# Two-layer HGRN2 and attention trunk in fp32r: the LayerNorms done by rows ahead of their transposes

## The chip, the cores and the metric

One core of one Trainium2 chip. The metric is the device time of one execution in microseconds (us). The kernel before takes 2177.33 us, the median of three runs (2177.27 to 2179.59).

## What is computed

The input x is one sequence of 1024 rows with 1024 channels in fp32. There are two layers. Each first mixes the rows (an HGRN2 recurrence in layer 0, sliding-window attention in layer 1), then applies a gated feed-forward network with 2816 hidden channels, and after both comes a residual with a LayerNorm:

```python
for layer in range(2):
    mix = hgrn2_mixer(h, ...) if layer == 0 else swa_sink_mixer(h, k_shared, v_shared, ...)
    h = layer_norm(ALPHA * h + mix, ln_mix_g[layer], ln_mix_b[layer])
    h = layer_norm(ALPHA * h + conv_ffn(h, ...), ln_ffn_g[layer], ln_ffn_b[layer])
    if layer == 0:
        k_shared, v_shared = split(h @ shared_w_kv)

def layer_norm(x, g, b):
    mu, var = x.mean(-1), square(x - mu).mean(-1)
    return (x - mu) * rsqrt(var + 1e-5) * g + b
```

So there are four LayerNorms: the mix norm and the end norm of either layer. g and b have one value for each channel.

## The kernel before, in words

Rows lie on partitions in eight blocks `tb` of 128 rows. The tile `Y` holds them as eight columns of 1024 channels. For a product the rows have to be turned: TensorE transposes each 128x128 piece into PSUM (L182), and the turned block is written to SBUF, with channels on partitions. Every fp32 product is done as three fp32r matmuls (L172 high x high, L173 with a low part of one operand, L174 with that of the other). `split` (L198) makes the two parts: a cast on ACT (L199) gives the high part and a subtraction on DVE (L147) the low part. A piece of weights costs the same two instructions.

The order of time is: the HGRN2 mixer; `out_proj` of layer 0 with the mix norm; `Up` (the first feed-forward product, 2 x 11 column pairs `fc`); `Down` (the second); keys and values; attention; then `out_proj`, `Up` and `Down` of layer 1. `Up` and `Down` use a Strassen-Winograd form with seven block products each, so DVE also forms sums of blocks of weights and of turned rows. TensorE runs in an order written out in the program; a list `od` of small tasks interleaves transposes with matmuls, each task due at a given matmul time. Inside keys, values and attention DVE, ACT and POOL are in written order too; elsewhere a scheduler orders them. SP issues nearly all transfers, in order.

**The mix norm, `out_proj` (L317) and `Up.ln` (L370).** `out_proj` makes the second 512 columns of the blocks in the order tb = 4, 5, 6, 7, 0, 1, 2, 3. For each block DVE adds the residual (L340), takes statistics (L213) and spawns `Up.ln`: L219 and L220 finish them, and POOL raises the variance to the power -1/2 (L221). Then the rows are normalised in place, without g and b: for tb 4 to 7 POOL forms -mu/sigma (L229, L230) and ACT applies it (L231), and for tb 0 to 3 DVE does it in two pieces (L235). SP stores the block to DRAM as `ynd` (L373). Eight matmul times later TensorE turns the block into two PSUM banks (L182), and ACT writes the turned block with eight activations of 128x128 (L247) that apply g and b, which are now one scalar per partition (`par`). The splits and Winograd sums of turned blocks follow. The weights of `fc` = 0 and 1 are split beforehand (`weight_load`, `weight_sums`); two of their pieces lie in the tile `HT`.

**The residual of the second norm.** `ynd` has no g and b, so `Down.run` (L638) loads g and b as rows broadcast over partitions (two transfers of 512 KB), reloads each `ynd` block and applies the rows on DVE with two instructions of 128x1024 per block (L645), sixteen in a layer, between Down's first products. Down's evacuations (L597, L601) add the products to it.

**The end norms.** In layer 0 `ln_mid` (L252) normalises a block with L235, turns it in two halves, and writes each half with two activations on ACT (L247) and two `tensor_scalar` on DVE (L249), which apply g and b; then it splits it into `T` for keys and values. The residual gets its g and b in the attention part by `ln_rows` (L263): 32 instructions of 128x512 on DVE (L268). In layer 1 `ln_last` (L273) writes the output with two `scalar_tensor_tensor` of 128x1024 for each block (L279: subtract mu, multiply by the row g; L282: multiply by 1/sigma, add the row b).

Of the kernel before, what the change touches and what calls it, by code (L numbers as in the profile page):

```python
# [85 lines left out]
def trunk(ctx: ExitStack, tc: tile.TileContext, a: dict, out: bass.AP):  # L86
# [25 lines left out]
    rbd = drp.tile([16, 2 * P], F32, name="rbd")  # L112
    bsd = [drp.tile([P, FF // 256, 2, D], F32, name=f"bsd{l}") for l in range(2)]
# [13 lines left out]
    tail, place = {}, {}  # L127
# [96 lines left out]
    def ln_normal(tb, on_scalar=False):  # L224
        y = Y[:, tb, :]
        mv, rs = ln_stats(tb)
        if on_scalar:
            ms = sm.tile([P, 1], F32, name="ms")
            nc.gpsimd.tensor_scalar(ms, mv[:, 0:1], -1.0, None, op0=ALU.mult)  # L229
            nc.gpsimd.tensor_tensor(ms, ms, rs, op=ALU.mult)  # L230
            nc.scalar.activation(y, y, AF.Identity, bias=ms, scale=rs)  # L231
            return
        for q in range(2):
            yq = y[:, q * 512:(q + 1) * 512]
            nc.vector.tensor_scalar(yq, yq, mv[:, 0:1], rs, op0=ALU.subtract, op1=ALU.mult)  # L235

    def ln_turn(tb, hf, gcol, bcol, banks, on_vector=0, halves=range(2)):

        for q in halves:
            ps = banks(q)  # L240
            for k in range(4):
                tr(ps[:, k * P:(k + 1) * P], Y[:, tb, (4 * q + k) * P:(4 * q + k + 1) * P])
            for k in range(4):
                kc = 4 * q + k
                shift, scale = par[:, bcol + kc:bcol + kc + 1], par[:, gcol + kc:gcol + kc + 1]
                if k < 4 - on_vector:
                    nc.scalar.activation(hf[:, kc, :], ps[:, k * P:(k + 1) * P], AF.Identity, bias=shift, scale=scale)  # L247
                else:
                    nc.vector.tensor_scalar(hf[:, kc, :], ps[:, k * P:(k + 1) * P], scale, shift,  # L249
                                            op0=ALU.mult, op1=ALU.add)  # L250

    def ln_mid(tb, gcol, bcol):  # L252
        ln_normal(tb)
        yield 11.0 if tb < 4 else 18.0
        hf = place["hf"](tb)
        for q in range(2):
            ln_turn(tb, hf, gcol, bcol, lambda _: psax()[:, :512], 2, (q,))
            if q == 0:
                yield 1.2
        ts = slice(tb * P, (tb + 1) * P)  # L260
        split(T[:, 0, :, ts], T[:, 1, :, ts], hf)

    def ln_rows(tbs, rows, wait, spill):  # L263
        for tb in tbs:
            for h in range(2):
                y = Y[:, tb, h * 512:(h + 1) * 512]
                for r, op in zip(rows, (ALU.mult, ALU.add)):
                    nc.vector.tensor_tensor(y, y, r[h], op=op)  # L268
                if h:
                    nc.sync.dma_start(spill[:, tb, :], Y[:, tb, :])  # L270
                yield wait

    def ln_last(tb, rows):  # L273
        y = Y[:, tb, :]
        mv, rs = ln_stats(tb)
        n = 1 if tb < NB - 1 else 2
# [4 lines left out]
        for hs in parts:  # L281
            nc.vector.scalar_tensor_tensor(y[:, hs], y[:, hs], rs, rows[1][:, hs], op0=ALU.mult, op1=ALU.add)  # L282
            nc.sync.dma_start(out[0, tb * P:(tb + 1) * P, hs], y[:, hs])
# [79 lines left out]
    class Up:  # L363
        def __init__(self, l, pool, rx):
            self.l, self.rx = l, rx
            self.wv = a["ffn_w_in"][l].rearrange("(kc p) c -> p kc c", p=P)
            self.TX = pool.tile([P, 3, 2, 4, 512], F32R, name="TX")
            self.W, self.raw, self.pieces = {}, {}, 0

        def ln(self, tb, gcol, bcol):  # L370
            with urgent():
                ln_normal(tb, tb > 3)
                nc.sync.dma_start(ynd[:, tb, :], Y[:, tb, :])  # L373
# [4 lines left out]
            with urgent():  # L378
                for q in range(2):
                    ln_turn(tb, hf, gcol, bcol, lambda _: psmm(), halves=(q,))  # L380
                    if tb < 4:
                        ks = slice(4 * q, 4 * q + 4)
# [21 lines left out]
        def weight_load(self, fc):  # L404
# [7 lines left out]
            for r in (r1, r2):  # L412
                j = self.pieces % (4 if fc > 1 else 3)
# [10 lines left out]
        def weight_sums(self, fc):  # L424
# [9 lines left out]
            split(blocks(2, 0), blocks(2, 1), r2)  # L434
# [50 lines left out]
        def run(self, ready, down):  # L485
# [7 lines left out]
            od.finish(ready[4:])  # L493
            mm = [psmm() for _ in range(4)]
# [25 lines left out]
    class Down:  # L520
# [117 lines left out]
        def run(self, mid_rows, end_rows, ln):  # L638
            self.later = []
            rows = row_tiles([self.free_rows(3 + j) for j in range(2)], *mid_rows)  # L640

            def shift(tb, r, op):
                if r is rows[0]:
                    nc.sync.dma_start(Y[:, tb, :], ynd[:, tb, :])
                tt(Y[:, tb, :], Y[:, tb, :], r, op=op)  # L645

            for tb in (0, 4, 1, 5, 2, 6, 3, 7):
                for r, op in zip(rows, (ALU.mult, add)):
                    self.later.append(lambda tb=tb, r=r, op=op: shift(tb, r, op))
            for i in range(7):  # L650
                for n, _ in enumerate(self.product(i, ln)):
                    if n % 4 == 3 and 44 * i + n > 8 and self.later:
                        self.later.pop(0)()
                    if i == 5 and n == 20 and end_rows is not None:
# [11 lines left out]
    with tc.tile_pool(name="t", bufs=1, reuse_waits="tile") as raws, hgrn_pool as hp:  # L666
# [48 lines left out]
        with tc.tile_pool(name="ep", bufs=1, reuse_waits="tile") as ep:  # L715
# [20 lines left out]
            with tc.manual_schedule(engines={EN.PE, EN.SP, EN.Activation, EN.DVE}):  # L736
                for i, n in enumerate(("hgrn_lb_logits", "ln_mix_g", "ln_mix_b", "ln_ffn_g", "ln_ffn_b")):
                    nc.scalar.dma_start(pr[16 * i:16 * (i + 1), :], a[n].rearrange("r (k p) -> (r k) p", p=P))
                nc.scalar.dma_start(pr[80:81, :], a["hgrn_gnorm_w"])
                nc.scalar.copy(warm, nhalf)  # L740
# [678 lines left out]
```

## Time and profile before

| | |
|---|---|
| median of three runs | 2177.33 us |
| the profiled execution's own time | 2176.27 us |
| its span in the trace | 2174.5 us |
| busy: PE / DVE / ACT / POOL | 2142.3 / 1735.6 / 917.1 / 186.2 us |
| granted TensorE clock | 0.999 |
| stages, roughly | layer 0 mixer to 470; out_proj and mix norm to 600; Up to 1000; Down to 1200; keys, values, attention to 1455; out_proj and mix norm to 1560; Up to 1950; Down to 2174.5 |

The engines are PE (TensorE matmul), DVE (VectorE), ACT (ScalarE), POOL (GpSimd) and SP (which issues transfers). A row of the groups gives a line of the program, its engine and operation, what is written from what, its shape and count, and behind the bar its busy time, the mean of one in ns, and the idle time before it with what ended it. A row of the waits reads: who waited <- for what: us in total, times, longest us. A row of the windows gives, for a stretch A:B, its length and then the busy time of PE, PEld, DVE, ACT and POOL, the granted clock, and the share and rate of the DMA.

### The profile page before, as it was taken

To read this page: it belongs to the slowest core of one execution; us is meant where nothing else is said; L and a number is where in the kernel's file an instruction comes from. 1 tells how busy PE (TensorE), PEld (TensorE's weight loads), DVE (VectorE), ACT (ScalarE), POOL (GpSimd) and SP (SyncE) were. 2 spreads that over 40 slices of the span, in tenths; PEclk is the share of its full clock that TensorE was granted. 3 is DMA by queue.
4 is the path that set the end of the run, shared out by engine and by line. 5 is a ranking of instruction groups with operands and counts; after the bars stand their busy time and mean duration, and the time that the engine had idled before them with its cause. 6 is when DMAs were issued, how large, how long until landed. Compare 5 with 4: busy or idle time off the path is not lost.

```text
span 2174.5 us, 32559 instructions
## 1 busy us (share of the span) xinstructions
PE 2142.3 (99%) x12879; PEld 1779.7 (82%) x12879; DVE 1735.6 (80%) x2281; ACT 917.1 (42%) x1535; POOL 186.2 (9%) x207
## 2 busy tenths in 40 slices
PE   8999999999999999999999999999999999999998
PEld 8788888878788888888888887778888888888887
DVE  3777666466789888889998766758899988889987
ACT  3333333243744443344443346755644444443431
POOL 0222121211100000000000022311000000000002
PEclk9999999999999999999999999999999999999999
DMA  5555443222222222228854331123133222249563
GB/s 198 194 195 180 151 175 121 69 88 93 90 80 91 84 78 87 87 97 270 291 170 136 106 100 35 35 97 117 59 109 96 87 79 76 79 163 327 198 216 128
DMA packets 225556, 278.97 MB, mean 128 GB/s; under 512 B 29721, under 2 KB 154362, under 8 KB 222586
## 3 DMA queue, kind: packets, MB, share of 16 engines
q1 hardware_dynamic: 224952, 276.76, 38.1%
q8 instruction: 101, 1.65, 0.3%
q14 instruction: 53, 0.43, 0.1%
q10 hardware_dynamic: 450, 0.12, 0.0%
HBM read 213.90 MB, written 62.93 MB: 127 GB/s over the span
## 4 chain that ended last, share of the span: by engine, by line
PE 77%; DVE 13%; DMA 3%; ACT 3%; issue 2%; POOL 1%; SPq 0%; ACTq 0%; DVEq 0%; POOLq 0%
PE psmm L172 16%; PE psmm L174 16%; PE psmm L173 16%; PE psax L172 7%; PE psax L174 7%; PE psax L173 7%; PE psax L178 3%; DVE T L147 2%; DVE HL L147 2%; PE psmm L178 2%; PE psax L1216 1%; PE psax L182 1%; DVE Y L477 1%; ACT T L199 1%; ACT Y L247 1%
## 5 line engine op out<-in xcount | busy, mean ns | idle before, releaser
L172 PE MATMUL psmm<-T,HL 128*128 128x512 f32 x896 | 358.2, 400 | 0.0
L173 PE MATMUL psmm<-T,HL 128*128 128x512 f32 x896 | 349.2, 390 | 2.8 <-DVE T L147 2.8
L174 PE MATMUL psmm<-T,HL 128*128 128x512 f32 x896 | 349.5, 390 | 0.0
L477 DVE SCALAR_TENSOR_TENSOR Y<-Y,cwt 128x1023 f32<-128x1023 f32 (+1 forms) x176 | 225.0, 1278 | 39.6 <-ACT Y L475 39.4
L475 ACT ACTIVATE Y<-Y,cwt 128x1024 f32<-128x1024 f32 x88 | 108.9, 1238 | 257.5 <-DVE Y L464 254.4
L173 PEld LDWEIGHTS psmm<-T,HL 128*128 128x128 f32 x896 | 168.6, 188 | 35.8 <-DVE T L147 3.5
L172 PEld LDWEIGHTS psmm<-T,HL 128*128 128x128 f32 x896 | 168.2, 188 | 36.1 <-issue 2.1
L174 PEld LDWEIGHTS psmm<-T,HL 128*128 128x128 f32 x896 | 168.1, 188 | 36.2
L199 ACT CAST HL<-rx 128x1024 fp32r<-128x1024 f32 (+1 forms) x137 | 140.4, 1046 | 113.1 <-DMA rx<-in_ffn_w_in_dram 31.4
L147 DVE TENSOR_TENSOR HL<-rx,HL 128x1024 fp32r<-128x1024 f32 (+1 forms) x137 | 165.4, 1210 | 12.9 <-ACT HL L199 12.3
L221 POOL TENSOR_TENSOR rs<-rs,nhalf 128x1 f32<-128x1 f32 x32 | 27.3, 854 | 1305.0 <-DVE rs L220 1304.7
L172 PE MATMUL psax<-T,HL 128*128 128x512 f32 x352 | 137.3, 390 | 0.0
L174 PE MATMUL psax<-T,HL 128*128 128x512 f32 x352 | 137.0, 389 | 0.0
L173 PE MATMUL psax<-T,HL 128*128 128x512 f32 x352 | 136.9, 389 | 0.0
L172 PE MATMUL psmm<-HL,T 128*128 128x256 f32 (+1 forms) x400 | 126.0, 315 | 0.0
L173 PE MATMUL psmm<-HL,T 128*128 128x256 f32 (+1 forms) x400 | 122.4, 306 | 1.0 <-DVE HL L147 0.9
L174 PE MATMUL psmm<-HL,T 128*128 128x256 f32 (+1 forms) x400 | 122.2, 306 | 0.1
L865 POOL TENSOR_TENSOR kp<-kp,tot 128x512 f32<-128x512 f32 x48 | 74.3, 1549 | 277.0 <-PE psax L178 139.9
L199 ACT CAST HT<-rx 128x1024 fp32r<-128x1024 f32 (+1 forms) x51 | 44.0, 862 | 88.5 <-PE psmm L173 29.9
L147 DVE TENSOR_TENSOR HL<-raw,HL 128x1024 fp32r<-128x1024 f32 x51 | 63.5, 1246 | 22.0 <-ACT HL L154 22.0
L172 PEld LDWEIGHTS psmm<-HL,T 128*128 128x128 f32 x400 | 76.9, 192 | 4.7 <-issue 1.2
L173 PEld LDWEIGHTS psmm<-HL,T 128*128 128x128 f32 x400 | 76.7, 192 | 4.8 <-DVE HL L147 1.7
(295 smaller groups left out, 5207.5 us busy)
## 6 DMA issues: line engine op xcount, KB each, us to landing
rx<-in_ffn_w_in_dram SPq DMA_DIRECT2D x136, 256.0 KB
rx<-gd SPq DMA_DIRECT2D x118, 256.0 KB
Y<-in_ffn_w_out_dram SPq DMA_DIRECT2D x44, 512.0 KB
bsd<-Y SPq DMA_DIRECT2D x22, 1024.0 KB
gd<-Y SPq DMA_DIRECT2D x44, 512.0 KB
raw<-in_hgrn_w_in_dram SPq DMA_DIRECT2D x32, 512.0 KB
rx<-in_ffn_w_out_dram SPq DMA_DIRECT2D x54, 256.0 KB
R<-bsd SPq DMA_DIRECT2D x44, 256.0 KB
```

Of the source, the lines that this page charges most:

```text
L147: make = lambda e: e.tensor_tensor(lo, src, hi.bitcast(F32), op=ALU.subtract)
L172: nc.tensor.matmul(ps, st(0), mv(0), start=start, stop=False)
L173: nc.tensor.matmul(ps, st(0), mv(1), start=False, stop=False)
L174: nc.tensor.matmul(ps, st(1), mv(0), start=False, stop=stop)
L178: nc.tensor.matmul(ps, lhsT, rhs, start=start, stop=stop, **kw)
L182: nc.tensor.transpose(ps, src, ident)
L199: nc.scalar.copy(hi, src)
L221: nc.gpsimd.tensor_tensor(rs, rs, nhalf, op=ALU.pow)
L247: nc.scalar.activation(hf[:, kc, :], ps[:, k * P:(k + 1) * P], AF.Identity, bias=shift, scale=scale)
L475: nc.scalar.activation(c, u, AF.Identity, bias=cwt[:, l, 3, ci:ci + 1], scale=cwt[:, l, 2, ci:ci + 1])
L477: nc.vector.scalar_tensor_tensor(c[:, sh:], u[:, :S - sh], cwt[:, l, 2 - sh, ci:ci + 1], c[:, sh:], op0=ALU.mult, op1=ALU.add)
L865: (nc.gpsimd if i else nc.vector).tensor_tensor(kv[:, :, 0, :], kv[:, :, 0, :], tv[:, :, 1:2].to_broadcast([P, nb, m]), op=ALU.mult)
```

## The change

All four norms go through one function, `ln_by_rows`: statistics as before, and then, while the block still has rows on partitions, two `scalar_tensor_tensor` of 128x1024 on DVE with g and b as broadcast rows (L238 and L241), and the store of the finished block: to `ynd`, to `h2d` or to the output. What is turned afterwards is finished, so ACT only copies it.

- At the start POOL issues two DRAM-to-DRAM transfers that copy ln_mix_g and ln_mix_b to `lmd`. `Up` loads its two rows from there into `HT` when it is made (two transfers of 512 KB on SP; in layer 1 they stand among the loads of the residual, ahead of those of the weights of `out_proj`).
- In `Up.ln` the instructions L229, L230, L231 and L235 go, and eight activations L247 give place to two copies of 128x512 (L345).
- `HT` holds the rows until the last block is normalised, so the last split of the weights of `fc` = 0 is put off (`self.last`) until after Up's products 4 and 5; the pieces of the raw weights are used in another order.
- In `Down.run` the row loads and L645 go; the eight reloads stay. The end norm's rows are loaded in product 5 in both layers.
- `ln_mid` turns a block in one piece of 128x1024 and splits it straight from PSUM; L247, L249, `ln_rows` with L268 and its row loads go.

TensorE's products are the same. The core of the diff:

```diff
-    def ln_normal(tb, on_scalar=False):
-        ...
-    def ln_turn(tb, hf, gcol, bcol, banks, on_vector=0, halves=range(2)):
-        ...
-    def ln_rows(tbs, rows, wait, spill):
-        ...
+    def ln_mid(tb):
+        yield 11.0 if tb < 4 else 18.0
+        ps = psax()
+        for kc in range(KC):
+            tr(ps[:, kc * P:(kc + 1) * P], Y[:, tb, kc * P:(kc + 1) * P])
+        ts = slice(tb * P, (tb + 1) * P)
+        split(T[:, 0, :, ts], T[:, 1, :, ts], ps.rearrange("p (k t) -> p k t", k=KC))
+
+    def ln_by_rows(tb, rows, dst, n=1):
         y = Y[:, tb, :]
         mv, rs = ln_stats(tb)
         parts = [slice(h * D // n, (h + 1) * D // n) for h in range(n)]
         for hs in parts:
             nc.vector.scalar_tensor_tensor(y[:, hs], y[:, hs], mv[:, 0:1], rows[0][:, hs],
                                            op0=ALU.subtract, op1=ALU.mult)
         for hs in parts:
             nc.vector.scalar_tensor_tensor(y[:, hs], y[:, hs], rs, rows[1][:, hs], op0=ALU.mult, op1=ALU.add)
-            nc.sync.dma_start(out[0, tb * P:(tb + 1) * P, hs], y[:, hs])
+            nc.sync.dma_start(dst[:, hs], y[:, hs])
...
             self.W, self.raw, self.pieces = {}, {}, 0
+            self.rows = [tail["R"][:, j, :].bitcast(F32) for j in range(2)]
+            for j in range(2):
+                nc.sync.dma_start(self.rows[j], bass.AP(tensor=lmd.tensor, offset=lmd.offset + (2 * j + l) * D,
+                                                        ap=[[0, P], [1, D]]))
-        def ln(self, tb, gcol, bcol):
+        def ln(self, tb):
             with urgent():
-                ln_normal(tb, tb > 3)
-                nc.sync.dma_start(ynd[:, tb, :], Y[:, tb, :])
+                ln_by_rows(tb, self.rows, ynd[:, tb, :])
             yield 8.0
...
                 for q in range(2):
-                    ln_turn(tb, hf, gcol, bcol, lambda _: psmm(), halves=(q,))
+                    ps, ks = psmm(), slice(4 * q, 4 * q + 4)
+                    for k in range(4):
+                        tr(ps[:, k * P:(k + 1) * P], Y[:, tb, (4 * q + k) * P:(4 * q + k + 1) * P])
+                    nc.scalar.copy(hf[:, ks], ps.rearrange("p (k t) -> p k t", k=4))
...
-            split(blocks(2, 0), blocks(2, 1), r2)
+            last = lambda: split(blocks(2, 0), blocks(2, 1), r2)
+            if fc:
+                last()
+            else:
+                self.last = last
...
             od.finish(ready[4:])
+            self.last()
             mm = [psmm() for _ in range(4)]
...
-        def run(self, mid_rows, end_rows, ln):
-            self.later = []
-            rows = row_tiles([self.free_rows(3 + j) for j in range(2)], *mid_rows)
-            ...
-                    self.later.append(lambda tb=tb, r=r, op=op: shift(tb, r, op))
+        def run(self, end_rows, ln):
+            self.later = [lambda tb=tb: nc.sync.dma_start(Y[:, tb, :], ynd[:, tb, :]) for tb in (0, 4, 1, 5, 2, 6, 3, 7)]
...
+                for i, n in enumerate(("ln_mix_g", "ln_mix_b")):
+                    nc.gpsimd.dma_start(lmd[i], a[n])
```

How the rows of the engines move, at three places. First DVE in the mix norm of layer 0, one block (`st`, `mv` and `rs` are the statistics; `HT` holds the broadcast rows; T<-Y,T is the low part of a turned block). Before:

```order
L340 SCALAR_TENSOR_TENSOR Y<-Y,psmm 128x512
L213 BN_STATS st<-Y 128x6
L147 TENSOR_TENSOR T<-Y,T 128x4x128
L219 BN_AGGR mv<-st 128x2
L387 TENSOR_TENSOR Y<-Y 128x512
L220 TENSOR_SCALAR rs<-mv 128x1
L235 TENSOR_SCALAR Y<-Y,mv,rs 128x512 x2
L147 TENSOR_TENSOR T<-Y,T 128x4x128
```

The same engine and place in the changed kernel (L299, L214, L220, L221 are L340, L213, L219, L220 of before, L148 is L147 and L351 is L387; HL<-rx is the low part of a piece of weights):

```order
L299 SCALAR_TENSOR_TENSOR Y<-Y,psmm 128x512
L148 TENSOR_TENSOR HL<-rx_4917,HL 128x1024
L148 TENSOR_TENSOR T<-Y,T 128x4x128
L214 BN_STATS st<-Y 128x6
L220 BN_AGGR mv<-st 128x2
L221 TENSOR_SCALAR rs<-mv 128x1
L238 SCALAR_TENSOR_TENSOR Y<-Y,mv,HT 128x1024
L148 TENSOR_TENSOR T<-Y,T 128x4x128
L241 SCALAR_TENSOR_TENSOR Y<-Y,rs,HT 128x1024
L351 TENSOR_TENSOR Y<-Y 128x512
```

The pair L235 has become L238 and L241, twice as long each, and one instruction of another block stands between them.

Second ACT at the same place (the turned blocks on their way out of PSUM, tb 6, 7 and 0). Before:

```order
L247 ACTIVATE Y<-psmm,par 128x128
L199 CAST T<-Y 128x4x128
L231 ACTIVATE Y<-Y,ms,rs 128x1024
L247 ACTIVATE Y<-psmm,par 128x128 x7
L199 CAST T<-Y 128x4x128
```

and in the changed kernel:

```order
L345 COPY Y<-psmm 128x512 x2
L200 CAST T<-Y 128x4x128 x2
L345 COPY Y<-psmm 128x512 x2
L200 CAST T<-Y 128x4x128 x2
L345 COPY Y<-psmm 128x512 x2
L200 CAST T<-Y 128x4x128 x2
```

Two copies stand where eight activations stood, and L231 is gone from between them.

Third DVE at the start of Down in layer 0 (L477 and L482 are the convolution and the gate of Up's last column pair; R holds the broadcast rows; T<-rx and HL<-rd are low parts of Down's operands). Before:

```order
L645 TENSOR_TENSOR Y<-Y,R 128x1024
L477 SCALAR_TENSOR_TENSOR Y<-Y,cwt 128x1023
L645 TENSOR_TENSOR Y<-Y,R 128x1024
L477 SCALAR_TENSOR_TENSOR Y<-Y,cwt 128x1022
L645 TENSOR_TENSOR Y<-Y,R 128x1024
L482 TENSOR_TENSOR Y<-Y 128x1024
L645 TENSOR_TENSOR Y<-Y,R 128x1024
L147 TENSOR_TENSOR HL<-rd,HL 128x1024
L147 TENSOR_TENSOR T<-rx_4913,T 128x1024
L645 TENSOR_TENSOR Y<-Y,R 128x1024 x3
```

and in the changed kernel (L445 and L450 are L477 and L482 of before):

```order
L445 SCALAR_TENSOR_TENSOR Y<-Y,cwt 128x1023
L148 TENSOR_TENSOR HL<-rd,HL 128x1024
L445 SCALAR_TENSOR_TENSOR Y<-Y,cwt 128x1022
L148 TENSOR_TENSOR T<-rx_4916,T 128x1024
L450 TENSOR_TENSOR Y<-Y 128x1024
L148 TENSOR_TENSOR T<-rx_4917,T 128x1024
L148 TENSOR_TENSOR HL<-rx_4915,HL 128x1024
L148 TENSOR_TENSOR T<-rd,T 128x1024
```

L645 is gone, and the splits stand next to the convolution.

More of the change, by code (lines that the diff above doesn't have):

```diff
@@ L112, in trunk @@
     rbd = drp.tile([16, 2 * P], F32, name="rbd")
+    lmd = drp.tile([2, 2, D], F32, name="lmd")
     bsd = [drp.tile([P, FF // 256, 2, D], F32, name=f"bsd{l}") for l in range(2)]
@@ L126, in trunk @@
     ring = {"hl": 4, "raw": 0}
-    tail, place = {}, {}
+    tail = {}
     def raw_tail(pool):
@@ L252, in ln_mid @@
[L252 to L261, printed above, removed]
-    def ln_rows(tbs, rows, wait, spill):
[L264 to L271, printed above, removed]
@@ L1105, in ffn @@
                 up = Up(l, pu, tail["raw"])
-                lns = out_proj(us, begun, rows, resid, up, lambda tb: up.ln(tb, gcol, bcol))
+                lns = out_proj(us, begun, rows, resid, up, up.ln)
                 up.run(lns, down)
@@ L1303, in trunk @@
             od.finish(lns[:4])
-            late = [od.spawn(ln_rows(range(1), rows, 2.5, h2d), 6.0)]
             k_part(0)
@@ L1307, in trunk @@
                 od.finish(lns[2 * tp:2 * tp + 2])
-                if tp == 2:
-                    late.append(od.spawn(ln_rows(range(1, NB), rows, 2.0, h2d)))
                 v_part(tp)
```

59 lines of the change are left out of this document (10 added, 49 removed).

## The prediction

> **What bounds the kernel now.** I read the page first, then the waits of TensorE by stage, then the windows, then the groups of the instructions that the change removes. The page says who can be helped at all.
>
> ```profile
> span 2174.5 us, 32559 instructions
> PE 2142.3 (99%) x12879; PEld 1779.7 (82%) x12879; DVE 1735.6 (80%) x2281; ACT 917.1 (42%) x1535; POOL 186.2 (9%) x207
> ```
>
> TensorE is idle for 2174.5 - 2142.3 = 32.2 us in all, and the change leaves its products alone. Work saved on DVE or ACT counts only where it shortens one of those idle times; work added counts where it makes a new one. So the next view is the waits of PE in the stages that the change touches. They are, in this order: the mix norm of layer 0 (524 to 600), the start of Down of layer 0 (1000 to 1120), its end norm with keys and values (1120 to 1300), the mix norm of layer 1 (1481 to 1560), and the start of Down of layer 1 (1950 to 2080).
>
> ```profile
> PE psmm L182 <- ACT Y L247: 1.7, 3, 0.7
> PE psmm L173 <- DVE T L147: 1.4, 1, 1.4
> PE psmm L182 <- DVE Y L340: 1.2, 1, 1.2
> ```
>
> ```profile
> PE psmm L173 <- DVE T L147: 0.8, 1, 0.8
> PE psax L172 <- DVE Y L601: 0.5, 1, 0.5
> PE psmm L172 <- ACT T L199: 0.4, 1, 0.4
> ```
>
> ```profile
> PE psax L182 <- DVE q L249: 1.4, 1, 1.4
> PE psax L182 <- DVE R L249: 1.1, 2, 0.6
> PE psax L182 <- ACT q L247: 0.8, 1, 0.8
> ```
>
> ```profile
> PE psmm L173 <- DVE T L147: 1.4, 1, 1.4
> PE psmm L182 <- ACT Y L247: 0.3, 1, 0.3
> ```
>
> ```profile
> PE psax L172 <- DVE Y L601: 0.9, 1, 0.9
> PE psmm L173 <- DVE T L147: 0.8, 1, 0.8
> PE psmm L172 <- ACT T L199: 0.4, 1, 0.4
> ```
>
> The five stages hold 4.3, 1.7, 3.3, 1.7 and 2.1 us, 13.1 us together. That is the most this change can win, 0.6% of the span. A measurement of this kernel can tell about 0.2%, here 4.35 us, from no change.
>
> How much slack DVE has where the change gives it work is in the windows (length, then busy time of PE, PEld, DVE, ACT, POOL; clock; DMA).
>
> ```profile
> 540.00:600.00 60.00, 55.68 (x269) 45.20 (x268) 43.86 (x77) 45.99 (x98) 7.60 (x12) 1.00 0.28 97
> 1000.00:1120.00 120.00, 118.34 (x520) 97.13 (x519) 116.97 (x126) 46.85 (x46) 0.00 (x0) 1.00 0.76 254
> 1495.00:1560.00 65.00, 63.29 (x310) 52.45 (x310) 50.30 (x87) 47.70 (x99) 7.76 (x13) 1.00 0.26 91
> 1950.00:2080.00 130.00, 128.03 (x563) 105.15 (x562) 125.71 (x135) 52.69 (x52) 0.00 (x0) 1.00 0.73 248
> ```
>
> In the two mix norms DVE idles for 16.1 of 60 and 14.7 of 65 us. At the two starts of Down it is busy for 97%. The change moves work from the full stretches into the looser ones.
>
> **The mix norms.** These groups carry the prices, the first two of ACT, the others of DVE; the last row shows two L282 in a row.
>
> ```profile
> L247 ACT ACTIVATE Y<-psmm,par 128x128 f32<-128x128 f32 x96 | 36.5, 467 | 3.8 <-PE psmm L182 2.7 <-DMA ynd<-Y 1.0
> L455 ACT COPY Y<-psmm 128x512 f32<-128x512 f32 x24 | 13.8, 574 | 2.3 <-PE psmm L174 2.3
> L231 ACT ACTIVATE Y<-Y,ms,rs 128x1024 f32<-128x1024 f32 x8 | 10.0, 1250 | 13.4 <-POOL ms L230 13.4
> L235 DVE TENSOR_SCALAR Y<-Y,mv,rs 128x512 f32<-128x512 f32 x32 | 16.0, 544 | 10.8 <-POOL rs L221 10.8
> L279 DVE SCALAR_TENSOR_TENSOR Y<-Y,mv,R 128x1024 f32<-128x1024 f32 x7 | 8.9, 1276 | 0.0
> 2144.33 2.48 DVE L282 SCALAR_TENSOR_TENSOR Y<-Y,rs,R 128x1024 f32<-128x1024 f32 x2
> ```
>
> L238 and L241 are what L279 and L282 are in the last norm, so a block costs DVE 2.48 us. Of blocks 4 to 7 nothing of this stood on DVE (ACT's L231 did it): +2.48 each. Of blocks 0 to 3 the pair L235 goes, 2 x 0.544: +1.4 each. A mix norm gains 4 x 2.48 + 4 x 1.4 = 15.5 us of DVE. ACT loses, per block, 8 x 0.467 = 3.7 us for two copies at the price of L455, 2 x 0.574 = 1.15 us; over eight blocks 20.7 us, and four L231, 5.0 us.
>
> ```profile
> 470.00:540.00 70.00, 68.26 (x450) 56.59 (x449) 42.15 (x67) 18.88 (x40) 9.94 (x10) 1.00 0.35 119
> 591.54 0.50 PE L173 MATMUL psmm<-T,HL 128*128 128x512 f32 x1 [1.41 <-DVE T L147]
> 1545.47 0.50 PE L173 MATMUL psmm<-T,HL 128*128 128x512 f32 x1 [1.36 <-DVE T L147]
> L199 ACT CAST TX<-rx 128x1024 fp32r<-128x1024 f32 x4 | 4.2, 1053 | 16.7 <-DMA rx<-in_swa_w_out_dram 16.7
> ```
>
> The first row is the stretch in which layer 0 loads its `HT` rows; the two of PE are the second matmul of Up's product 1 in either layer; the last is what ACT waits for the weights of `out_proj` in layer 1 (1445 to 1500).
>
> Layer 0: DVE 43.9 + 15.5 = 59.4 of 60. Layer 1: 50.3 + 15.5 = 65.8 of 65. The slack is used up, just covered in the first and just not in the second. But TensorE's waits there are mostly for ACT and for chains that go through ACT, and ACT becomes quick. I put the order rows of the changed kernel through a queue by hand, with these durations, a new DVE instruction starting 0.08 us before the end of the one ahead, and TensorE's rows kept at 6.34 us per block (estimates, all of them). In layer 0 the norm of a block is ready before TensorE comes to turn it for tb 4, 5 and 6, late by 1.7 us for tb 7, by 0.6 for tb 0, and by 0.7 each for tb 2 and 3; Up's product 1 would begin near 589.7 and find its low part ready, where now its second matmul goes at 591.5. The rows of `HT` go into a stretch in which the DMA is busy for 35%: nothing. **Layer 0: -1.3** (bounds -4.3, all of its waits, and +4). In layer 1 they (1 MB) go ahead of the weights of `out_proj`, for which ACT waits 16.7 us already, so DVE begins about 2 us later relative to TensorE; there tb 7 is late by 1.45, tb 0 by 0.45, tb 3 by 0.35, and the wait of the next block's PSUM bank adds some 0.7 three times, so that product 1 begins near 1547.6, where now its second matmul goes at 1545.5. **Layer 1: +2.2** (bounds -1.7 and +6).
>
> The split that is put off (one cast, one subtraction of 1.2 us) now stands on DVE behind the turned sums and four splits, some 10 us of work; TensorE has products 1 and 2 of both columns, 10.9 us, until product 6 of `fc` = 0 needs it. It is ready about 2 us early: nothing. If that cover is gone, it costs what DVE is late.
>
> A new wait stands in L345: the first copy of a turned block lies in the place from which `ynd` is stored, and has to wait for the store. It waits so now, too, once for 1.0 us (the row L247 above). Behind it ACT holds the casts of turned blocks and DVE their low parts. The store now leaves at the end of L241, as now at the end of L235 or L231; my queue has each copy ready 0.6 to 1 us before DVE wants it: nothing, with up to +1 per layer inside the bounds.
>
> POOL's power L221 is where a rule speaks against the change.
>
> ```profile
> 535.15 0.57 POOL L221 TENSOR_TENSOR rs<-rs,nhalf 128x1 f32<-128x1 f32 x1
> 547.69 1.22 DVE L147 TENSOR_TENSOR HL<-rx,HL 128x1024 fp32r<-128x1024 f32 x1
> 547.86 1.47 POOL L221 TENSOR_TENSOR rs<-rs,nhalf 128x1 f32<-128x1 f32 x1
> ```
>
> It takes 0.57 us in one place and 1.47 in the other, where DVE had begun a subtraction of two SBUF tiles (1.22 us) at 547.69. The power ended 0.42 us after that one, while DVE was at the next. After the change L238, which reads two SBUF tiles, always starts ahead of it, so L241 waits for it until 0.4 us after L238; in the mix norms one DVE instruction of 0.6 us or more stands between, which covers it. The Trainium skill says it more sharply ("SBUF — State Buffer", section "Who interferes with whom"): a DVE instruction with two SBUF inputs and a GpSimd instruction that reads SBUF exclude each other for the whole instruction, whichever came first. Held to the letter the power could lose to the instruction between as well, and L241 would be later by some 0.6 us per block; the row at 547.86 speaks for the short form, and the long form is in the slower rival.
>
> **The starts of Down.**
>
> ```profile
> L645 DVE TENSOR_TENSOR Y<-Y,R 128x1024 f32<-128x1024 f32 x32 | 38.3, 1218 | 0.6 <-DMA R<-in_ln_mix_g_dram 0.3 <-DMA Y<-ynd 0.2
> ```
>
> Sixteen of L645 go in each layer, 19.5 us of DVE where it is busy for 117.0 of 120 and 125.7 of 130, and 1 MB of row loads. TensorE waits there for low parts, casts and evacuations behind them, 1.7 and 2.1 us. With 19.5 us off a full queue I take most of it: **-3.0** for both (bounds -3.8 and 0; if the waits come from transfers, not from L645, nothing goes).
>
> **The end norm of layer 0, keys and values.**
>
> ```profile
> L268 DVE TENSOR_TENSOR Y<-Y,X 128x512 f32<-128x512 f32 x32 | 22.2, 718 | 0.6
> ```
>
> L268 goes with 22.2 us. A block trades two L235 for 2.48 us (+1.4), and four L249 and four L247 go; the block's eight transposes fill one PSUM tile, which is freed by a cast and a subtraction of 1024 instead of by two engines in turn. All 3.3 us of waits there are for L247 and L249, but the new tile is held for about 2.3 us by two engines one after the other, so a wait of its kind comes back: **-1.5** (bounds -3.3 and +1). The rows for this norm, 1 MB, load in product 5 of Down as layer 1 does now, behind all the waits of PE that its Down shows: nothing.
>
> **The start.** Two transfers on POOL's queue are new, and no transfer of this kernel stands there now.
>
> ```profile
> 0.72 0.42 ACTq L738 DMA_DIRECT2D pr<-in_hgrn_lb_logits_dram  x1
> 7.13 2.36 POOL L147 TENSOR_TENSOR HL<-raw,HL 128x1024 fp32r<-128x1024 f32 x1 [4.55 <-ACT HL L154]
> ```
>
> An issue on ACT's queue takes 0.42 us. Behind POOL's issues stands its first subtraction, ahead of which it idles for 4.55 us; two issues at this price are hidden, and `lmd` is read first at about 470 us. Bounds 0 and +2 (if they last longer than that idle time, TensorE's first products wait for the subtraction). The Trainium skill ("DMA: Bandwidth & Descriptors", section "Specifications") has about 1 us to the first byte for such a transfer; by it the sum stays as it is, an estimate that no run here shows.
>
> **The sum**, against the profiled execution: 2176.27 - 1.3 + 2.2 - 3.0 - 1.5 = 2172.67. The median shown lies 1.06 above that execution, so I forecast 2173.7. With half of each bound its own range is 2170 to 2177.5; chance 0.50, nearly evenly faster (0.24) and within 0.2% (0.26), since the edge is at 2172.97.
>
> **The rivals.**
>
> *DVE takes TensorE's place as the bound of both mix norms (slower).* Its waits there now, from 524 to 600, hold some that the change does not remove:
>
> ```profile
> DVE Y L235 <- POOL rs L221: 2.6, 4, 0.7
> DVE rx L429 <- DMA rx<-in_ffn_w_in_dram: 1.2, 1, 1.2
> DVE Y L340 <- PE psmm L174: 0.8, 2, 0.6
> ```
>
> If L241 waits for POOL as L235 does, and the rest stays, layer 0 needs 59.4 + 4.6 = 64.0 us for its 60, and layer 1, with the same 4.6, 70.4 for its 65: +9.4, less the 4.5 of Down and the end norm, 2181.2 against the execution and 2182.2 as a median. It decides from the point where more than half a microsecond of DVE's idle time in these stretches cannot be filled. For it: 59.4 and 65.8 leave nothing. Against it: the sums for later products can slide past the stretch. Chance 0.23 (0.20 slower, 0.03 within).
>
> *All waits that can go do go.* -4.3 in layer 0, 0 in layer 1, -3.8 in Down, -3.3 at the end norm: 2164.9, as a median 2165.9. For it: ACT is relieved by 26 us in a mix norm. Against it: DVE is full there. Chance 0.15.
>
> *The removed work was hidden anyway.* Down's waits are those of casts behind transfers and stay, the end norm gets its wait back: 2176.27 - 1.3 + 2.2 = 2177.2, as a median 2178.2. Chance 0.12, within 0.2%.
>
> **How the numbers follow.** Faster 0.24 + 0.15 = 0.39, within 0.26 + 0.03 + 0.12 = 0.41, slower 0.20. The range reaches from the second rival to a little past the first, 2165.5 to 2184, and leaves out some 0.15: worse pile-ups of DVE above, and half of the case of all waits below.
>
> **What would show it.** In the changed profile L345 should take 0.57 us and L238 1.28; DVE should be near 95% in both mix norms; PE's waits at L182 there should be for DVE (L241), around 3 us in layer 0 and 4 in layer 1; the waits of 0.8 and 0.4 us at the start of Down should be gone; in keys and values one wait of a microsecond for a low part should be left. Wrong I would be if L241 waits for POOL in the mix norms, if Up's product 6 waits for the split put off, if PE waits for L345 behind a store, or if the first products wait for POOL.

## The result: slower by 0.23%

The changed kernel takes 2183.34 us (median of 20 runs, 2179.98 to 2188.40) against 2178.49 (20 runs, 2175.65 to 2181.20): a ratio of 1.0023, 95% interval 1.0017 to 1.0030, slower by some 5 us where I had forecast a gain of 3.6. The profiled execution took 2179.98 us, the shortest of the twenty, with a span of 2178.2.

The head of its page answers to the two lines that the prediction began with.

```profile
span 2178.2 us, 32363 instructions
PE 2152.7 (99%) x12879; PEld 1780.0 (82%) x12879; DVE 1707.2 (78%) x2201; ACT 866.3 (40%) x1399; POOL 197.3 (9%) x193
```

DVE lost 28.4 us of work and ACT 50.8. TensorE's idle time fell from 32.2 to 2178.2 - 2152.7 = 25.5 us, even more than I had hoped for. Yet the span grew, because PE is now *busy* for 10.4 us longer, with the same 12879 matmuls. No wait can explain that; they have to take longer each.

The waits of PE by stage say the same. In the order of the prediction, the mix norm of layer 0 (one row), the mix norm of layer 1 (one row), and the start of Down of layer 1 (one row); the start of Down of layer 0 and its end norm have no wait left at all.

```profile
PE psmm L183 <- DVE Y L241: 1.9, 3, 1.3
PE psmm L183 <- DVE Y L241: 1.3, 3, 0.8
PE psax L173 <- DVE Y L570: 0.3, 1, 0.3
```

That is 3.5 us where there were 13.1. The windows of the same stretches show the work moved as drawn: DVE nearly full in the mix norm of layer 0, looser at the starts of Down.

```profile
540.00:600.00 60.00, 57.97 (x283) 47.10 (x282) 58.83 (x89) 29.33 (x48) 10.81 (x7) 1.00 0.23 89
1000.00:1120.00 120.00, 119.99 (x528) 98.68 (x528) 107.48 (x119) 53.17 (x52) 0.00 (x0) 1.00 0.80 271
1495.00:1560.00 65.00, 63.59 (x307) 51.66 (x306) 60.23 (x91) 29.69 (x49) 10.26 (x7) 1.00 0.29 103
1950.00:2080.00 130.00, 129.73 (x570) 106.70 (x570) 114.09 (x126) 56.39 (x56) 0.00 (x0) 1.00 0.77 261
```

The time is lost where the change does nothing: in Up, away from the norms. The window from 660 to 980, first of before and then of the changed kernel:

```profile
660.00:980.00 320.00, 320.00 (x1413) 265.06 (x1412) 288.23 (x324) 134.32 (x155) 0.00 (x0) 1.00 0.28 91
```

```profile
660.00:980.00 320.00, 320.00 (x1399) 262.20 (x1399) 287.35 (x323) 133.09 (x154) 0.00 (x0) 1.00 0.27 88
```

PE is busy for 320 of 320 us in both, at a granted clock of 1.00 in both, and does 14 matmuls fewer (1%). A busy engine hides this; the count beside it shows it. Which matmuls they are, the timeline shows: a product of twelve matmuls with TX streamed and HL loaded, its first and last row, in the kernel before,

```profile
757.95 0.39 PE L172 MATMUL psax<-TX,HL 128*128 128x512 f32 x1
...
760.44 0.39 PE L174 MATMUL psax<-TX,HL 128*128 128x512 f32 x1
```

and in the changed one, with a product of TX and HT ahead of it:

```profile
676.00 0.39 PE L173 MATMUL psmm<-TX,HT 128*128 128x512 f32 x1
...
678.50 0.39 PE L175 MATMUL psmm<-TX,HT 128*128 128x512 f32 x1
...
761.14 0.39 PE L173 MATMUL psax<-TX,HL 128*128 128x512 f32 x1
...
763.71 0.39 PE L175 MATMUL psax<-TX,HL 128*128 128x512 f32 x1
```

Eleven steps from start to start take 2.49 us before (0.2264 each) and 2.57 now (0.2336 each); with HT in place of HL they take 2.50 (0.2273). Starts are shown to 0.01 us, so such a step is good to about 0.001. The duration column reads 0.39 in all of them, since it is modelled; only the distance from start to start tells. (In the expectations below I wrote 0.2275 for the quick ones, read less finely.) Taking the same matmul in both traces, the changed kernel is 0.32 us late at the beginning of Up's product 6 in layer 0 (602.66 against 602.34) and 5.85 us late at the first matmul of Down (1022.88 against 1017.03); layer 1 loses another 4.5 us between the same two places.

Up is not alone. The second half of `out_proj` streams TX against pieces of T, and slowed as well. The first and the twelfth of these matmuls in layer 0, before and in the changed kernel (2.49 and 2.57 us for eleven steps):

```profile
524.14 0.39 PE L172 MATMUL psmm<-TX,T 128*128 128x512 f32 x1
...
526.63 0.39 PE L174 MATMUL psmm<-TX,T 128*128 128x512 f32 x1
```

```profile
526.21 0.39 PE L173 MATMUL psmm<-TX,T 128*128 128x512 f32 x1
...
528.78 0.39 PE L175 MATMUL psmm<-TX,T 128*128 128x512 f32 x1
```

What differs for TX is where the program's allocator put it. The changed kernel no longer has the scalar tile `ms`, two buffers of 32 bytes per partition, and every tile allocated behind it slid down by 64 bytes: TX from byte 178176 of each partition, a multiple of 2048, to 178112; HT from 153600 to 153536; and so the raw weights, Down's R and the attention tiles (two of which, q and X, were laid out anew besides). T, Y and HL lie ahead of `ms` and stayed. This is theory A; its rival, theory B, was that the spacing comes from the changed traffic of DVE and ACT.

### The profile page after: what moved, and what is told of

Its sections match the earlier page's. It is cut to its first block, busy times and chain, and to the rows that moved or that the text cites. A ratio compares the mean times of both kernels' runs of the same rounds, so it can differ in the third digit from the quotient of the medians.

```text
span 2178.2 us, 32363 instructions
## 1 busy us (share of the span) xinstructions
PE 2152.7 (99%) x12879; PEld 1780.0 (82%) x12879; DVE 1707.2 (78%) x2201; ACT 866.3 (40%) x1399; POOL 197.3 (9%) x193
## 4 chain that ended last, share of the span: by engine, by line
PE 80%; DVE 12%; DMA 4%; issue 2%; ACT 1%; SPq 0%; POOL 0%; ACTq 0%; DVEq 0%; POOLq 0%
PE psmm L173 16%; PE psmm L175 16%; PE psmm L174 16%; PE psax L173 8%; PE psax L175 8%; PE psax L174 8%; PE psax L179 3%; DVE T L148 2%; PE psmm L179 2%; PE psax L1171 1%; DVE HL L148 1%; PE psax L183 1%; DMA rx<-in_ffn_w_in_dram 1%; PE psmm L183 1%; DVE Y L238 1%
## 5 line engine op out<-in xcount | busy, mean ns | idle before, releaser
L445 DVE SCALAR_TENSOR_TENSOR Y<-Y,cwt 128x1023 f32<-128x1023 f32 (+1 forms) x176 | 225.0, 1278 | 39.9 <-ACT Y L443 39.6
L148 DVE TENSOR_TENSOR HL<-rx,HL 128x1024 fp32r<-128x1024 f32 (+1 forms) x137 | 165.1, 1209 | 18.0 <-ACT HL L200 17.8
L222 POOL TENSOR_TENSOR rs<-rs,nhalf 128x1 f32<-128x1 f32 x32 | 46.3, 1448 | 1411.3 <-DVE rs L221 1411.3
L148 DVE TENSOR_TENSOR HL<-raw,HL 128x1024 fp32r<-128x1024 f32 x51 | 63.5, 1245 | 34.4 <-ACT HL L155 34.4
L173 PEld LDWEIGHTS psmm<-HL,T 128*128 128x128 f32 x400 | 77.0, 193 | 5.0 <-issue 1.2
L174 PEld LDWEIGHTS psmm<-HL,T 128*128 128x128 f32 x400 | 76.8, 192 | 4.5 <-DVE HL L148 1.3
L175 PEld LDWEIGHTS psmm<-HL,T 128*128 128x128 f32 x400 | 76.8, 192 | 4.4 <-DVE T L148 1.2
```

The source lines that it names most:

```text
L148: make = lambda e: e.tensor_tensor(lo, src, hi.bitcast(F32), op=ALU.subtract)
L173: nc.tensor.matmul(ps, st(0), mv(0), start=start, stop=False)
L174: nc.tensor.matmul(ps, st(0), mv(1), start=False, stop=False)
L175: nc.tensor.matmul(ps, st(1), mv(0), start=False, stop=stop)
L222: nc.gpsimd.tensor_tensor(rs, rs, nhalf, op=ALU.pow)
L445: nc.vector.scalar_tensor_tensor(c[:, sh:], u[:, :S - sh], cwt[:, l, 2 - sh, ci:ci + 1], c[:, sh:], op0=ALU.mult, op1=ALU.add)
```

## The experiments

All comparisons are with the kernel before on the same chip; medians and ratios are of 5 to 11 runs where there are several.

**The tiles put back** (e1_pad): the changed kernel, 64 bytes of padding more.

```diff
-    cp.tile([P, 104], F32, name="pad1")
+    cp.tile([P, 120], F32, name="pad1")
```

> The changed kernel with 64 bytes of padding more per partition, so that every large tile lies where it lay before. Theory A (the place of the tiles): the scalar tile `ms` went, all tiles behind it slid down by 64 bytes, and matmuls that stream from TX now follow each other every 0.2333 us instead of 0.2275; with the padding the spacing in Up is 0.2275 again, the two Up stages lose about 4.5 us each, and the time is about 9 to 10 us under the changed kernel's 2183.3, near 2173 to 2174, 4 to 5 us under the kernel before. Theory B (the spacing follows from the other work on DVE and ACT, not from addresses): no change, 2183, spacing 0.2333.

2173.99 us against 2177.94, a ratio of 0.9983 (0.9974 to 0.9992). The window of Up has its matmuls again:

```profile
660.00:980.00 320.00, 320.00 (x1413) 264.96 (x1413) 288.23 (x325) 135.01 (x155) 0.00 (x0) 1.00 0.28 89
```

Sixteen floats of padding turn the change from 5 us slower to 4 us faster (0.17%: less than the 0.2% that the prediction counted as a change, but the interval leaves out 1). B falls: DVE has the same 2201 instructions as in the changed kernel and ACT the same 1399. The tiles q and X of the attention are not back at their addresses of before, but they lie as before modulo 512 bytes.

**The kernel before, shifted** (e2_shift):

```diff
-    cp.tile([P, 104], F32, name="pad1")
+    cp.tile([P, 88], F32, name="pad1")
```

> The kernel before with 64 bytes of padding fewer, so that its tiles lie where the changed kernel has them; nothing else differs. Theory A: the spacing of matmuls that stream from TX rises to 0.2333 us, about 9 to 10 us more than the kernel before, near 2188. Theory B: no change against before, 2178.5.

2187.67 us, a ratio of 1.0045 (1.0032 to 1.0058): +9.7 us, without any of the change.

```profile
660.00:980.00 320.00, 320.00 (x1400) 262.20 (x1399) 288.16 (x324) 133.44 (x154) 0.00 (x0) 1.00 0.27 87
```

**TX alone put back** (e3_tx):

```diff
+            pool.tile([P, 16], F32, name="pad2")
             self.TX = pool.tile([P, 3, 2, 4, 512], F32R, name="TX")
```

> The changed kernel with 64 bytes of padding ahead of TX alone: TX is back in its old place, HT, the raw weights, Down's R and the attention tiles stay 64 bytes lower. Theory A with TX as the streamed operand at fault: nearly all of the loss goes, within 1.5 us of the kernel with all tiles in place. If the stationary pieces in HT or the targets of transfers are at fault: the spacing stays at 0.2333 for some products and half or more of the 9 us stays. Theory B: 2183.

2178.40 us, a ratio of 1.0002 (0.9993 to 1.0010): half of the loss came back, not nearly all. Products of TX and HL are quick again (0.2264), but those of TX and HT, quick in the changed kernel, now take 0.2291 (2.52 us for eleven steps):

```profile
676.22 0.39 PE L173 MATMUL psmm<-TX,HT 128*128 128x512 f32 x1
...
678.74 0.39 PE L175 MATMUL psmm<-TX,HT 128*128 128x512 f32 x1
```

So it was not TX's place as such. HT explains some 1.5 us of the 4.4 that are left against e1_pad (0.75 in each Up). Of the rest the profiles show only single pieces: against e4_late (below) this one is 0.9 us later at 470 us, loses 1.0 more in the mix norm of layer 0, and idles for 2.7 us in Down of layer 1 where e4_late idles for 0.9. Why, I did not trace.

**Four other distances, in the kernel before**: TX alone higher by 32, 128 and 512 bytes (d1_tx32, d2_tx128, d3_tx512: `pool.tile([P, 8], ...)`, 32 and 128 floats ahead of TX), and the mixer's raw weights by 64 bytes (d4_raw).

```diff
+            pool.tile([P, 8], F32, name="pad2")
             self.TX = pool.tile([P, 3, 2, 4, 512], F32R, name="TX")
```

```diff
+        raws.tile([P, 16], F32, name="pad2")
+        hp.tile([P, 112], F32, name="pad3")
         raw_tail(raws)
```

> The kernel before with TX alone 32 bytes higher (178208 instead of 178176), to see which step of the address matters. If any distance from the place of 2048 bytes costs the same: matmuls that stream from TX every 0.2333 us, as at 64 bytes. If the cost follows the distance: about 0.230. If only steps of 64 bytes count: worse than at 64, or not at all.

> The kernel before with TX alone 128 bytes higher. If what counts is that a row of 2048 bytes crosses a 2048-byte line: 0.2333 us again. If a multiple of 128 bytes suffices: 0.2275, the time of before.

> The kernel before with TX alone 512 bytes higher. If a row of 2048 bytes that crosses a 2048-byte line is slow whatever the step: 0.2333 us. If the low bits of the address count (anything under 512): 0.2275.

> The kernel before with the three tiles that receive layer 0's weights 64 bytes higher, and the other tiles of the mixer at other multiples of 512. The three profiles with these tiles 64 bytes lower were 1.7 to 2.1 us late at 30 us of the span, those with them in place 0 to 0.8. If transfers into shifted rows are slower: 1.3 to 2 us late at 30 us. If that was the scatter of the first loads: 0 to 0.8.

One run each, beside 2177.00 of before: 2190.64, 2187.05, 2179.36 and 2176.84. The windows of Up at 32, 128 and 512 bytes:

```profile
660.00:980.00 320.00, 320.00 (x1390) 260.70 (x1389) 286.40 (x322) 133.67 (x154) 0.00 (x0) 1.00 0.27 86
```

```profile
660.00:980.00 320.00, 320.00 (x1395) 261.48 (x1394) 286.16 (x321) 131.75 (x152) 0.00 (x0) 1.00 0.28 88
```

```profile
660.00:980.00 320.00, 320.00 (x1414) 264.96 (x1413) 288.40 (x325) 135.37 (x156) 0.00 (x0) 1.00 0.28 89
```

With TX 32 or 128 bytes off, its products with HL and with HT both step by 0.233 us; at 512 all step by 0.2264 again, although a row of TX then crosses a 2048-byte line. The low bits count, below 512; a distance of 256 was not tried. Shifted raw weights cost nothing: 0.8 us late at 30 us of the span, within the 0 to 1.7 that profiles with all tiles in place show there (d3_tx512 has the 1.7).

**Everything shifted, and HL alone** (f1_all, f2_hl), to tell the place of the streamed operand from the agreement of the two. In f1_all the padding at the very start is cut, so T, Y and HL go down by 64 bytes with the others; in f2_hl HL goes up by 64, with the small tiles behind it (`ident` for the transposes, scalars), and nothing else.

```diff
-    cp.tile([P, 224], F32, name="pad0")
+    cp.tile([P, 208], F32, name="pad0")
```

```diff
+    cp.tile([P, 16], F32, name="pad2")
     HL = cp.tile([P, 12 * 1024], F32R, name="HL")
...
-    cp.tile([P, 104], F32, name="pad1")
+    cp.tile([P, 88], F32, name="pad1")
```

> The kernel before with every tile 64 bytes lower, T, Y and HL too (padding at the very start 64 bytes shorter). The products of the changed kernel that were slow had their streamed and their loaded operand at different distances from a 512-byte line (TX shifted, HL not: 0.2334 us; T and HL unshifted: about 0.227; TX and HT both shifted: 0.2274). If the absolute address of the streamed operand counts: all products slow, T, HL and TX alike at 0.2333 us, some 25 us or more above before. If the two operands only have to agree modulo 512: spacing 0.2265 to 0.2275 everywhere and the time of before, 2177 to 2180.

> The kernel before with HL (and the small tiles behind it) 64 bytes higher; T, TX and HT in place. If the two operands have to agree: products of T or TX with HL at 0.2333 us, those of TX with HT at 0.2265; Up slower by about 10 us per layer, and the mixer and Down with it, 2200 or more. If only the streamed operand's place counts: Up as before, 0.2265; Down slower only where it streams from HL.

f1_all: 2179.14 against 2177.67, a ratio of 1.0005 (0.9996 to 1.0014). f2_hl: 2203.76, one run. Their windows of Up, and the ends of one product of T and HL in f2_hl:

```profile
660.00:980.00 320.00, 320.00 (x1414) 264.96 (x1413) 288.43 (x326) 134.79 (x156) 0.00 (x0) 1.00 0.28 89
```

```profile
660.00:980.00 320.00, 320.00 (x1380) 258.96 (x1379) 284.33 (x319) 132.88 (x153) 0.00 (x0) 1.00 0.26 83
```

```profile
657.98 0.39 PE L173 MATMUL psmm<-T,HL 128*128 128x512 f32 x1
...
660.55 0.40 PE L175 MATMUL psmm<-T,HL 128*128 128x512 f32 x1
```

With every tile 64 bytes off, nothing is lost. With HL alone off, products of T with HL slow down too (2.57 us for eleven steps), although T has not moved. What counts is how the streamed and the loaded operand lie to each other, not where either lies: agreement modulo 512 bytes is enough, and each of the other distances tried (32, 64 and 128 bytes) costs time.

**The copy of the rows moved** (e4_late: e1_pad with the two transfers issued by SP in the middle of layer 0):

```diff
-                for i, n in enumerate(("ln_mix_g", "ln_mix_b")):
-                    nc.gpsimd.dma_start(lmd[i], a[n])
...
             yield 320.0
+            for i, n in enumerate(("ln_mix_g", "ln_mix_b")):
+                nc.sync.dma_start(lmd[i], a[n])
```

> The changed kernel with all tiles in place and the copy of the rows of g and b to DRAM issued by SP in the middle of layer 0 instead of by POOL at the start. If the two transfers on POOL's queue hold up the first loads (2.0 us later at 30 us in the one profile of the changed kernel): 1 to 2 us under the kernel that only has its tiles in place. If that was the scatter of the start from run to run: within 0.7 us of it.

2173.33 us, a ratio of 0.9984 (0.9975 to 0.9993): no different from e1_pad. The transfers on POOL's queue cost nothing that can be measured.

**The rows of HT loaded behind out_proj's weights** (v1_rows: e4_late with the loads of `Up.__init__` moved into a method).

```diff
                 elif dh == 0 and tb == 4:
+                    ff.load_rows()
                     ff.weights(0)
```

> The changed kernel with its tiles in place, the copy to DRAM in the middle of layer 0, and the two row loads into HT put behind the loads of out_proj's weights on SP. In the profiles with the rows ahead, ACT's first cast of those weights in layer 1 comes 3.6 us later against TensorE than before, and the mix norm of layer 1 costs 2.3 us. If the late weights cause it: 1.5 to 2.5 us under the version without this move (2173.3), near 2171.5. If DVE's longer norm alone causes it: the same 2173.3 within 0.7.

2173.81 us, a ratio of 0.9982 (0.9973 to 0.9991), the same as e4_late. ACT's wait for those weights, first in the changed kernel, then in v1_rows:

```profile
L200 ACT CAST TX<-rx 128x1024 fp32r<-128x1024 f32 x4 | 4.2, 1055 | 19.8 <-DMA rx<-in_swa_w_out_dram 19.8
```

```profile
L200 ACT CAST TX<-rx 128x1024 fp32r<-128x1024 f32 x4 | 4.2, 1052 | 16.7 <-DMA rx<-in_swa_w_out_dram 16.7
```

In e4_late ACT's wait is 19.7 us, so the weights come 3 us earlier in v1_rows. The mix norm of layer 1 still costs 1.9 us (2.8 in e4_late, 2.3 in e1_pad): by these profiles the late weights cost at most 0.9 us, and the median shows none of it. Of my two readings the second came: DVE's longer norm costs most of that time, and 2.9 us of TensorE's waits from 1481 to 1600 in v1_rows are for L241.

**The end norm of layer 0 alone** (g_end: the kernel before, with only that norm done by rows).

```diff
     def ln_next(tb, down):
-        return ln_mid(tb, 48, 64)
+        ln_last(tb, [down.free_rows(j) for j in range(2)], h2d[:, tb, :])
+        return ln_mid(tb)
...
-            late = [od.spawn(ln_rows(range(1), rows, 2.5, h2d), 6.0)]
```

> The kernel before with the end norm of layer 0 alone done by rows (its rows loaded in Down's product 5, one turned piece of 1024, no L268); the mix norms and Down's residual as before, all tiles in place. By the stages of the aligned runs this part is worth -4.2 us and the mix norms with Down together about 0: then 2178 - 4 = 2174. By my prediction's terms it is worth -1.5: then 2176.5.

2173.84 us, a ratio of 0.9985 (0.9976 to 0.9994). This part alone brings what the whole change brings with its tiles in place. The mix norms by rows and the shorter starts of Down together bring nothing that can be told from zero.

## Why the prediction was wrong, step by step

The forecast of 2173.7 is what the change gives with its tiles in place (2173.99 and 2173.33). That agreement is in part luck: by the table below the end norm gave 2.7 us more than its term, and the others together 1.8 us (e4_late) to 5.4 us (e1_pad) less. The forecast was wrong by a term that was not in the sum.

**The step that failed** is the first: "the change leaves its products alone", and with it "TensorE's rows kept at 6.34 us per block". I took the instructions and their order as all that a change can alter in TensorE's work. The diff removed a scalar tile, the allocator moved TX and HT against HL and T, and in Up the products of TX with HL, those of the odd column pairs, slowed by 3% and some of T with HL by less: 5.5 us in layer 0 (1.1 of it waits) and 4.5 in layer 1. The slower products of TX and T lengthen the end of `out_proj` too: in e2_shift, which has the shift alone, that stretch costs 0.6 us more than before in layer 0 and 0.4 in layer 1. It could have been seen: the kernel carries tiles named pad0 and pad1 that no instruction reads, and the removed lines include an allocation. No rival of mine had it; the slower rival was right in sign for a reason that did not happen.

The other terms, from the same matmul in the trace of before and in that of e1_pad (e4_late behind it), so without the shift. The two columns are one execution each: e1_pad's profiled one took 2177.24 us, the slowest of its eleven, and e4_late's 2173.09, near its median.

| stretch | forecast | e1_pad | e4_late |
|---|---|---|---|
| mix norm of layer 0, to Up's product 6 | -1.3 | -1.6 | -2.3 |
| the same, with what comes back by 650 us | | +0.1 | -1.0 |
| end norm of layer 0, keys and values | -1.5 | -4.2 | -4.2 |
| mix norm of layer 1, to 1600 us | +2.2 | +2.3 | +2.8 |
| Down, both layers | -3.0 | +0.9 | -2.1 |

*The mix norms.* In layer 0 the size was right up to product 6, and 1.3 to 1.7 us came back right behind it: PE waits there for low parts of weights (0.7 us for HT, 0.4 for HL in the changed kernel) and, in e1_pad, 0.4 for a cast. DVE's sums did slide past the stretch, as the slower rival's counter-argument said, and were late there. In layer 1 the size was right and the reason half wrong: the late weights had a part in the forecast that v1_rows does not show.

*POOL's power.* It takes 1.45 us nearly everywhere now, 0.85 in the mean before, since L238 always stands ahead of it; and in the mix norms L241 waits for it for 0.4 us in all. That is one of the signs by which I said I would be wrong; it cost TensorE next to nothing. The row of the group L222 and that of L241 on `HT`, in the changed kernel:

```profile
L222 POOL TENSOR_TENSOR rs<-rs,nhalf 128x1 f32<-128x1 f32 x32 | 46.3, 1448 | 1411.3 <-DVE rs L221 1411.3
L241 DVE SCALAR_TENSOR_TENSOR Y<-Y,rs,HT 128x1024 f32<-128x1024 f32 x16 | 20.5, 1278 | 0.4 <-POOL rs L222 0.4
```

So the power runs behind the instruction with two SBUF operands, as the Trainium skill has it ("SBUF — State Buffer", section "Who interferes with whom"). In 15 of the 16 blocks of the mix norms it does not lose to the next one as well: it takes 1.44 to 1.53 us, the instruction between covers it, and the short form holds. In one block the long form came, and that is the whole wait of L241:

```profile
556.60 1.28 DVE L238 SCALAR_TENSOR_TENSOR Y<-Y,mv,HT 128x1024 f32<-128x1024 f32 x1
556.84 2.05 POOL L222 TENSOR_TENSOR rs<-rs,nhalf 128x1 f32<-128x1 f32 x1 [6.42 <-DVE rs L221]
557.80 0.69 DVE L148 TENSOR_TENSOR T<-Y,T 128x512 fp32r<-128x512 f32 x1
558.92 1.29 DVE L241 SCALAR_TENSOR_TENSOR Y<-Y,rs,HT 128x1024 f32<-128x1024 f32 x1 [0.43 <-POOL rs L222]
```

The power ended 0.40 us after L148, the second instruction with two SBUF operands. What decides between the two forms, the runs do not tell.

*The new wait for the store of `ynd`.* It came, and larger than I had it: 13.1 us of ACT, up to 3.2 at a time. It stayed hidden: no wait of PE is for L345.

```profile
L345 ACT COPY Y<-psmm 128x512 f32<-128x512 f32 x24 | 12.9, 589 | 13.1 <-DMA ynd<-Y 13.1
```

*The end norm.* The term was mis-sized, beyond its bound. All 3.3 us of waits went, no new one came, and the eight transposes in one go keep PE for less, so the waits of PE were not "the most this change can win": in keys and values 64 of them were busy for 9.7 us before and for 8.3 in e1_pad.

```profile
L182 PE MATMUL psax<-ident,Y 128*128 128x128 f32 x64 | 9.7, 274 | 3.3 <-DVE q L249 1.4 <-DVE R L249 1.1 <-ACT q L247 0.8
```

```profile
L183 PE MATMUL psax<-ident,Y 128*128 128x128 f32 x64 | 8.3, 272 | 0.0
```

I had let a wait of about a microsecond come back because two engines hold the larger PSUM tile in turn; it did not.

*Down.* The waits at its starts went, as forecast: by the same matmuls each layer gains 1.7 us there. In the changed kernel nothing took their place, but with the tiles in place PE is earlier, and waits in a later product for an evacuation on DVE: 1.0 us in layer 0 and 2.8 in layer 1 in e1_pad. In layer 1 DVE itself waits there for reloads of `gd` (the second row, from 2000 to 2080). I take it that a slower TensorE had hidden this; no run shows it, and the wait differs from one execution to the next (0.9 us in layer 1 in e4_late, 2.8 in v1_rows).

```profile
PE psax L173 <- DVE Y L570: 3.8, 2, 2.8
```

```profile
DVE rx L544 <- DMA rx<-gd: 2.8, 2, 2.2
```

*The start and the split put off* cost nothing that these runs show: the two issues on POOL's queue took 0.75 and 0.49 us where 0.42 each was forecast, e4_late, without them, is no faster than e1_pad, and product 6 of `fc` = 0 does not wait. The 0.7 us for HT above are in product 6 of `fc` = 2, in both layers; no run separates the split put off from DVE's other late work as their cause.

## What to carry to other kernels

Where a change adds, removes or resizes a tile, compare the addresses of all tiles behind it before anything else, and above all how each pair of streamed and loaded operands stands modulo 512 bytes (a shorter period was not tried); a tile of four bytes per partition, gone, cost twice what the change won. Read TensorE's speed from matmuls counted in a window and from the distance of starts, not from its busy share or the durations. And price the parts apart: here one of four brought the whole gain.

## What the runs showed of the hardware

- Matmuls of 128x512 in fp32r follow each other every 0.2264 us when both operands lie alike modulo 512 bytes. With the streamed tile 64 bytes lower than the loaded one, or 32 or 128 higher, it was 0.233 us; with it 64 bytes higher (TX and HT in e3_tx) 0.2291. The sign seems to count; why, and whether other distances under 512 are free, the runs do not tell. With all tiles 64 bytes off it was 0.2264 to 0.2273.
- The change from one pair to the next counts too. T and HL did not move in the changed kernel, but behind a product of TX and HT, both 64 bytes lower, their first ten steps take 0.231 us (2.31 in the rows below) and the rest 0.226 (2.94 for thirteen). That holds for all such places in the two Ups; in e1_pad and in f1_all, where all these tiles lie alike, the first ten take 0.2267.

```profile
678.73 0.39 PE L173 MATMUL psmm<-T,HL 128*128 128x512 f32 x1
...
681.04 0.39 PE L174 MATMUL psmm<-T,HL 128*128 128x512 f32 x1
...
683.98 0.39 PE L175 MATMUL psax<-T,HL 128*128 128x512 f32 x1
```

- A wait of 2.8 us in the midst of steady matmuls can cost more than itself. In e1_pad TensorE idled until 2069.2, and the granted clock of the windows around it fell to 0.66 and 0.94:

```profile
2064.00:2068.00 4.00, 2.41 (x11) 1.67 (x9) 2.98 (x4) 0.00 (x0) 0.00 (x0) 1.00 0.42 147
2068.00:2072.00 4.00, 2.77 (x7) 2.19 (x8) 3.35 (x5) 0.00 (x0) 0.00 (x0) 0.66 0.77 251
2072.00:2078.00 6.00, 6.00 (x26) 4.92 (x25) 3.67 (x5) 2.70 (x3) 0.00 (x0) 0.94 0.00 1
```

  v1_rows shows the same behind a wait of 2.8 us at the same place (0.63 and 0.96); in e3_tx a wait of 2.7 us there left the clock at 1.00. So it does not always come.

- The first 30 us scatter by up to 2 us from run to run. TensorE waits there for the loads of x, for 5.6 to 6.2 us in the changed kernel, e1_pad, e4_late, v1_rows and g_end; whether the scatter is theirs is not shown. The four profiles with the tiles from `ms` on 64 bytes lower (the changed kernel, e2_shift, e3_tx, f1_all) lie at 1.7 to 2.2, the nine with them in place at 0 to 1.7. d4_raw speaks against the raw weights as the cause; whether another tile is, stays open.
